# The last 1024 columns of a load as three loads of 96, 24 and 8 rows, in an add + GELU kernel on Trainium2

## The chip, the cores and the metric

The kernel runs on one core of a Trainium2 chip. The metric is the device time of one execution in microseconds (us), the median of several runs. Of the core's engines, four matter here: VectorE (DVE in the profile), ScalarE (ACT), GpSimd (POOL) and SyncE (SP), which only issues DMAs in this kernel. 16 DMA engines move data between HBM, where the inputs and the output lie, and SBUF, the memory that the engines work on, which has 128 rows (partitions).

## What is computed

Two float32 arrays of 1024 x 4096 are added, and the sum goes through the tanh form of GELU:

```python
z = x + y
return 0.5 * z * (1 + np.tanh(np.sqrt(2 / np.pi) * (z + 0.044715 * z ** 3)))
```

That is 33.55 MB read and 16.78 MB written.

## The kernel before, in words

Each array is seen as 128 rows of 32768 columns (L88): row p holds eight consecutive rows of the array, so a row's columns are contiguous in HBM. `zt` in SBUF holds a whole array (128 KB a row) and `yt` half of one (64 KB a row). Six DMAs, each of 128 rows by 16384 columns (64 KB a row, 8.39 MB), move everything, and all are issued by SyncE in this order (L169 to L171):

1. y, first half, into `yt` (load_y, L135)
2. x, first half, into `zt` (load_x, L130)
3. x, second half, into `zt` (L130)
4. y, second half, into `yt`, over the first half; it waits until all adds of the first half have read `yt`
5. store of the first half of `zt` (L139), after its last GELU
6. store of the second half, after its last GELU

The first two are moved ahead of the program's starting barrier (`begin_early`, L9), and the end of the program waits for the last store apart from everything else (`wait_late`, L23).

The work between is cut into 20 chunks of columns, mostly 2048 wide (L94); the last three are of 1024, 512 and 512. For each chunk an add makes z = x + y in place in `zt` (L150), on VectorE or, for chunks 7, 8 and 12, on GpSimd; then ScalarE applies GELU in place (L162). For eight chunks ScalarE first copies x into PSUM (L143), and the add reads it from there (`copies`, L95). The order on every engine is written out by hand (L96 to L98, L169 to L174), and a semaphore ends each wait. A DMA engine works off its share of the DMAs in the order in which they were issued.

Which loads a chunk waits for is worked out from the column ranges of the loads (`over`, L111, and `needs`, L176). The two functions that matter for the change:

```python
xloads = [HALF, HALF]                                     # L91
def load_x(i):                                            # L128
    a, b = xr[i]
    nc.sync.dma_start(out=zt[:, a:b], in_=xv[:, a:b])     # L130
```

Of the kernel before, what the change touches and what calls it, by code (L numbers as in the profile page):

```python
# [66 lines left out]
def kernel(  # L67
# [12 lines left out]
    nc = tc.nc  # L80
    P = nc.NUM_PARTITIONS
# [6 lines left out]
    xv, yv, ov = (a.rearrange("(p n) d -> p (n d)", p=P) for a in (x, y, out))  # L88

    HALF = TOT // 2  # L90
    xloads = [HALF, HALF]  # L91
    yloads = [16384, 16384]
    stores = [16384, 16384]
    chunks = [1024, 1024] + [2048] * 7 + [512, 1536] + [2048] * 6 + [1024, 512, 512]  # L94
# [6 lines left out]
    def ranges(sizes):  # L101
        ends = [sum(sizes[: i + 1]) for i in range(len(sizes))]
        assert ends[-1] == TOT
        return [(e - f, e) for e, f in zip(ends, sizes)]

    xr, yr, sr, cr = (ranges(r) for r in (xloads, yloads, stores, chunks))
# [4 lines left out]
    def over(rs, lo, hi):  # L111
        return [i for i, (a, b) in enumerate(rs) if a < hi and b > lo]
# [6 lines left out]
    zt = pool_sb.tile([P, TOT], fp32, tag="z", name="z")  # L119
# [7 lines left out]

    def load_x(i):  # L128
        a, b = xr[i]
        nc.sync.dma_start(out=zt[:, a:b], in_=xv[:, a:b])  # L130

    def load_y(i):
        a, b = yr[i]
# [30 lines left out]
    def earlier_user(c):  # L164
        lo, hi = copies[c], copies[c] + chunks[c]
        before = [k for k in copies if k < c and copies[k] < hi and copies[k] + chunks[k] > lo]
        return [(add, k) for k in before]

    sp = [(load_y, i) for i in over(yr, 0, HALF)] + [(load_x, 0), (load_x, 1)]  # L169
    sp += [(load_y, i) for i in over(yr, HALF, TOT)]  # L170
    sp += [(store, i) for i in range(len(stores))]  # L171
    pool = [(add, c) for c in on_gpsimd]
# [4 lines left out]
        load_x: lambda i: [],  # L177
        load_y: lambda i: [(add, c) for c in over(cr, yr[i][0] - HALF, yr[i][1] - HALF)],
        copy: lambda c: [(load_x, i) for i in over(xr, *cr[c])] + earlier_user(c),
        add: lambda c: [(load_x, i) for i in over(xr, *cr[c])]  # L180
        + [(load_y, i) for i in over(yr, *cr[c])]
        + [(copy, k) for k in copies if k == c]
# [56 lines left out]
```

## Time and profile before

| what | value |
|---|---|
| median of 3 runs | 120.08 us (119.96 to 120.28) |
| profiled execution, first to last instruction (span) | 118.7 us; no other time of it is given |
| VectorE busy | 29.1 us (25%) |
| ScalarE busy | 44.1 us (37%) |
| GpSimd busy | 13.8 us (12%) |
| adds, 128x2048, both operands in SBUF, VectorE | 2.28 us each |
| GELUs, 128x2048 | 1.90 us each |
| SyncE waits before its issue of the second y load | 53.2 us |
| SyncE waits before the two stores | 41.9 us in all, the longest 21.9 |

The page of a profile shows one execution: busy time of each engine, the span in 40 equal slices (each digit is the busy share in tenths; the DMA row is the mean over the 16 DMA engines), the DMA queues with their packets, the chain of work that ended last, and groups of instructions. The chain is followed back from the last instruction: at each step to what released it. Behind the page lies the trace. It lists each instruction, each update of a semaphore, and each DMA packet with its start, its duration and its size, though not the DMA engine that moved it. Where a landing is given, it is the time from the issue of a DMA to the last update of its semaphore.

### The profile page before, as it was taken

To read this page: it belongs to the slowest core of one execution; us is meant where nothing else is said; L and a number is where in the kernel's file an instruction comes from. 1 tells how busy PE (TensorE), PEld (TensorE's weight loads), DVE (VectorE), ACT (ScalarE), POOL (GpSimd) and SP (SyncE) were. 2 spreads that over 40 slices of the span, in tenths; PEclk is the share of its full clock that TensorE was granted. 3 is DMA by queue.
4 is the path that set the end of the run, shared out by engine and by line. 5 is a ranking of instruction groups with operands and counts; after the bars stand their busy time and mean duration, and the time that the engine had idled before them with its cause. 6 is when DMAs were issued, how large, how long until landed. Compare 5 with 4: busy or idle time off the path is not lost.

```text
span 118.7 us, 112 instructions
## 1 busy us (share of the span) xinstructions
DVE 29.1 (25%) x18; ACT 44.1 (37%) x30; POOL 13.8 (12%) x7
## 2 busy tenths in 40 slices
DVE  0000000000000099994000000009999920000000
ACT  5000000000000096792059999903799980000000
POOL 0000000000000029980000000009500000000000
DMA  9889988998899888998899888998899888988891
GB/s 353 353 375 641 398 353 353 596 464 353 353 420 618 376 353 353 618 442 353 353 508 552 353 353 375 641 398 353 353 552 508 353 353 353 707 353 353 353 641 66
DMA packets 864, 50.33 MB, mean 424 GB/s; under 512 B 96, under 2 KB 96, under 8 KB 96
## 3 DMA queue, kind: packets, MB, share of 16 engines
q1 hardware_dynamic: 864, 50.33, 98.5%
HBM read 33.55 MB, written 16.78 MB: 424 GB/s over the span
## 4 chain that ended last, share of the span: by engine, by line
DMA 56%; DVE 14%; ACT 10%; DVEq 1%; ACTq 0%; SPq 0%; issue 0%
DMA z<-in_x_dram 34%; DMA y<-in_y_dram 21%; DVE z L150 14%; ACT z L162 10%; DVEq L206 1%; ACTq L206 0%; SPq L135 0%; DVEq L150 0%
## 5 line engine op out<-in xcount | busy, mean ns | idle before, releaser
L162 ACT ACTIVATE z<-z 128x2048 f32<-128x2048 f32 (+3 forms) x20 | 29.7, 1555 | 5.5 <-DVE z L150 5.5
L143 ACT COPY ps<-z 128x2048 f32<-128x2048 f32 (+2 forms) x8 | 13.0, 1654 | 46.8 <-DMA z<-in_x_dram 45.1
L150 DVE TENSOR_TENSOR z<-z,y 128x2048 f32<-128x2048 f32 (+2 forms) x9 | 13.6, 1574 | 40.0 <-DMA z<-in_x_dram 40.0
L150 DVE TENSOR_TENSOR z<-ps,y 128x2048 f32<-128x2048 f32 (+2 forms) x8 | 15.6, 2016 | 25.4 <-DMA y<-in_y_dram 25.4
L150 POOL TENSOR_TENSOR z<-z,y 128x2048 f32<-128x2048 f32 x3 | 13.5, 4529 | 70.7 <-DVE z L150 43.4
L191 ACT ACT_TABLE_LOAD x1 | 1.3, 1283 | 1.3 <-PEq L223 1.3
L190 DVE MEMSET one<- 128x1 f32 x1 | 0.1, 59 | 1.3 <-PEq L223 1.3
L191 ACT ACTIVATE one<-one 128x1 f32<-128x1 f32 x1 | 0.2, 203 | 0.0
L223 POOL MEMSET const-float32-0.0<- 128x1 f32 x1 | 0.1, 99 | 0.2 <-issue 0.2
L223 POOL MEMSET const-bfloat16-1.0<- 128x1 bf16 x1 | 0.1, 102 | 0.0
L223 POOL MEMSET const-uint8-127<- 128x1 uint8 x1 | 0.1, 102 | 0.0
L223 POOL MEMSET const-float32-1.0<- 128x1 f32 x1 | 0.1, 99 | 0.0
## 6 DMA issues: line engine op xcount, KB each, us to landing
y<-in_y_dram SPq DMA_DIRECT2D x2, 23.6
z<-in_x_dram SPq DMA_DIRECT2D x2, 50.1
out_dram<-z SPq DMA_DIRECT2D x2, 21.6
```

The lines of the kernel that those rows point to most:

```text
L143: nc.scalar.copy(out=in_psum(c), in_=zt[:, a:b])
L150: ins = eng.tensor_add(out=zt[:, a:b], in0=first, in1=yt[:, o : o + b - a])
L162: nc.scalar.activation(out=zt[:, a:b], in_=zt[:, a:b], func=act.Gelu_apprx_tanh)
L190: nc.vector.memset(one[:, :1], 0.0)
L191: nc.scalar.activation(out=one[:, :1], in_=one[:, :1], func=act.Gelu_apprx_tanh)
L206: tc.compile()
L223: nc = _bacc.Bacc("TRN2", target_bir_lowering=False, num_devices=1)
```

## The change

The second x load is cut into a load of 15360 columns and a rest of 1024 columns. The load of 15360 columns still has all 128 rows (60 KB a row). The rest is issued as three DMAs of 96, 24 and 8 rows, with 4 KB a row, before the second y load:

```diff
     HALF = TOT // 2
-    xloads = [HALF, HALF]
+    xloads = [HALF, 15360, 1024]
...
     def load_x(i):
         a, b = xr[i]
-        nc.sync.dma_start(out=zt[:, a:b], in_=xv[:, a:b])
+        parts = [(0, P)] if b - a > 1024 else [(0, 96), (96, 120), (120, P)]
+        for f, e in parts:
+            nc.sync.dma_start(out=zt[f:e, a:b], in_=xv[f:e, a:b])
...
-    sp = [(load_y, i) for i in over(yr, 0, HALF)] + [(load_x, 0), (load_x, 1)]
+    sp = [(load_y, i) for i in over(yr, 0, HALF)] + [(load_x, 0), (load_x, 1), (load_x, 2)]
```

On SyncE the one issue becomes four, with no wait among them; no other engine's instructions move. The add of chunk 18 (512 columns), its GELU and the second store wait for the three small loads; everything else of the second half waits for the load of 15360 columns or for none. Two things follow from the number of DMAs: the first copy of the second half waits for the shorter load, and GpSimd clears the semaphores at the end in two instructions instead of one (L47).

## The prediction

> **What bounds the kernel now.** I read the table in 40 slices first, then the queue totals, then the chain that ended last in order of time, then the issues on SyncE with their landings, and last the packet records of the trace, listed by start.
>
> The page, its slices and queue totals:
>
> ```profile
> span 118.7 us, 112 instructions
> ...
> DMA  9889988998899888998899888998899888988891
> ...
> DMA packets 864, 50.33 MB, mean 424 GB/s; under 512 B 96, under 2 KB 96, under 8 KB 96
> ...
> q1 hardware_dynamic: 864, 50.33, 98.5%
> ```
>
> The DMA row is never below 8 until the last slice, and the packets fill 98.5% of the 16 DMA engines' time: six transfers of 8.39 MB, one behind the other, with no hole. The 864 packets are 768 of 64 KB (one row of a transfer each) and 96 of 4 bytes, one for each DMA engine and transfer. So a transfer is 128 rows, 8 for each of 16 DMA engines.
>
> The chain that ended last (start us, us, what), and the stores' line (issue to landing):
>
> ```profile
> 0.43 40.89 DMA z<-in_x_dram
> ...
> 41.42 13.37 DVE z L150 x7
> ...
> 54.86 25.15 DMA y<-in_y_dram
> ...
> 84.72 11.86 ACT z L162 x7
> ...
> 97.09 0.52 ACT z L162
> ```
>
> ```profile
> L139 SPq DMA_DIRECT2D out_dram<-z x2: 343/346/348, 77.2 to 97.6; - x2
> ...
> DMA to landing us min/median/max: 21.0/21.6/22.2
> ```
>
> The first x load lands at 0.43 + 40.89 = 41.3, the second y load at 80.0, the stores at 77.2 + 22.2 = 99.4 and 97.6 + 21.0 = 118.6, where the span ends. These landings lie about 19.3 us apart, however early the transfer was issued. The chain runs through VectorE and ScalarE only because each issue waits for them: the second y load is issued at 54.9, while the x load before it moves until 60.7; the last store at 97.6, while the first store moves until 99.4.
>
> The packet records say how tight that is. A 64 KB packet takes 2.418 us, and packets on one DMA engine start 2.414 to 2.417 us apart (27.1 GB/s); 8 x 2.414 = 19.31 is the spacing above. A DMA engine that is late stays late: at the first full packets they start 0.716 us apart from first to last, at the last packets 0.478 us. The last 4-byte packet starts at 118.31, its signal comes at 118.64. One place has a little slack of its own: the last store's first packets start at 98.49, 0.88 after its issue at 97.61, and three of the DMA engines waited some 0.1 us for it; the latest one didn't wait. So the time is that of the DMA engine that ends last, and everything in this forecast is about how many ns that one gains or loses.
>
> **The change, part by part.**
>
> SyncE. One x load becomes four, so three more issues. The timeline has 0.33 to 0.42 us for one of SyncE's issues: they end near 1.6 + 3 x 0.4 = 2.8 us. The next thing on SyncE is the second y load, which waits for the adds until 54.8: 52 us hide them. If that cover were gone, they would cost some 1.2 us.
>
> Waits that move. The main part of the second x load is 15360 of 16384 columns, so it lands 1024 / 16384 x 19.3 = 1.2 us earlier, near 59.5, and ScalarE's copies (start 60.74) with it. ScalarE then ends its seven long gelus 1.2 us sooner and the first store is issued near 76 instead of 77.2; it stands in the queue behind the second y load until 80, so nothing comes of it. VectorE's adds after that wait for the y load at 80.0, as before. The three small loads (near 60.7 to 62) are waited for by the second last add of 512 columns, near 95, and by the last store: over 30 us of cover. GpSimd has one more clearing of semaphores at the end, which waits for all but the last store; that store moves for 19 us beside it.
>
> Bytes. None more or less. But eight rows of 64 KB a DMA engine become eight of 60 KB and, for 128 rows of 4 KB, new shares. A 4 KB row at the rate above is 2.414 / 16 = 0.151 us. Whole rows in equal numbers mean 6 rows on each of 16 DMA engines for the 96; for the 24, which 16 does not divide, 2 rows on 12 (or 3 on 8); for the 8, 1 row on 8. I take 12 and 8: 6 + 2 + 1 = 9 rows on eight of them, 8 on four, 6 on four, where all had 8. No row of before shows a load of fewer rows; the bounds are equal shares still (0) and 6 + 3 + 1 = 10 rows (+0.302).
>
> What limits a DMA engine is the open question, and it sets the sign. In every transfer of before, a DMA engine works on its own eight rows, so 27.1 GB/s can be the limit of the engine or that of the place in SBUF which those eight rows share. Both fit every packet here.
>
> - If the engine is the limit: +0.151 us for nine rows, 0 for eight, -0.302 for six. This is the lower bound.
> - If the place is the limit, 27.1 GB/s for each group of eight rows: 24 rows are three groups' worth and 8 rows one, and a second DMA engine on the same group gains nothing. With groups of eight consecutive rows, the 96, the 24 and the 8 would each take 8 x 0.151 = 1.207 us for a DMA engine that has part in all three: 3.62 where it had 1.207, so +2.41. This is the upper bound.
>
> Between +0.15 and +2.41 no row of before is nearer to one end. Groups so scattered that 8 consecutive rows meet eight of them are as special as groups wholly in a block; I take the middle, **+1.28**, for the most delayed DMA engines. Both ends stay in the range.
>
> [...]
>
> Small packets. Three more transfers bring up to three more 4-byte packets (9 ns each) to a DMA engine, and eight more row packets. What a packet costs beside its bytes is not seen; nothing below, and the 9 ns of the 4-byte packet above: 0 to 0.1 us; I take 0.05.
>
> Who is last. If the late DMA engines are those with six rows, the delayed ones start from up to 0.48 us of lead. That is worth 0 to 0.4; I take 0.2 off.
>
> No cover remains behind this: all three transfers that follow are full, so a lag goes to the end unchanged. The second y load lands later by it, the adds, the gelus and the last store's issue too, and the first store ends later by the same, so the 0.88 us from issue to first packet stays covered as now.
>
> Sum: 1.28 + 0.05 - 0.20 = +1.13 us. The profiled execution has 118.68 from its first to its last instruction, and no other time of it is given; 119.8 is the span I expect. The median of the three runs is 120.08, so I count 1.4 us around the span, unchanged: 120.08 + 1.13 = **121.2 us**.
>
> **The rivals.**
>
> *The engine is the limit and the shares fit (the other side).* The place is the end of the last transfers: the last four DMA engines end 0.282, 0.385, 0.394 and 0.478 us behind the first, the other twelve within 0.214. If those four are the ones with six rows they come to 0.176 at most, and the nine-row ones, if they are the eight earliest, to 0.099 + 0.151 = 0.250: the end moves from 0.478 to 0.250, -0.23 us, and with 0.05 for packets -0.18: 119.9. It decides as soon as the late four are the lightened four; if instead a late one has nine rows, it is +0.15 + 0.05: 120.3. For it: a clean step in the records between twelve and four. Against it: no record says which DMA engine is which, and the limit must be wholly the engine's.
>
> *The change does not do what it says.* Each row stays with the DMA engine that has it in a full load; then all keep eight rows, and only the packets remain: +0.05, 120.1. For it: one engine on its own eight rows is all that before shows.
>
> *Place-bound and worse.* Rows dealt out in an order in which the DMA engines crowd on one group at a time: the upper bound and more, +2.4 to +4: 122.5 to 124. Against it: it needs them to be in step, while the records show them up to 0.7 us apart.
>
> **Chances.** Place-bound as summed 0.57, own range 120.7 to 122.0; engine-bound 0.28 (119.85 to 120.35); equal shares 0.08 (120.1); crowded 0.07. The range takes the first three: 119.85 to 122.0. A measurement of this kernel tells about 0.3%, 0.36 us, from no change: beyond 120.44 slower, under 119.72 faster. Faster: even the best balance is -0.23, so only what I have not thought of, 0.04. Same: most of engine-bound, equal shares and a small part of the first, 0.33. Slower: 0.63.
>
> **What would show it.** Landings: the second y load at 81.1 instead of 80.0 and both stores later by as much say place-bound; 79.8 to 80.2 says engine-bound or equal shares. In the packet records, 4 KB packets of 0.3 us or longer say that a destination is shared; 0.151 to 0.16 that it isn't. Their count by DMA engine shows the shares. The spread of the last packets, 0.478 now, grows beyond 0.8 if the nine-row engines are held up and shrinks to 0.25 if the shares fit. It would all be wrong if a hole opened in the DMA row near 60 us, or if the last store were issued after the first one's end.

## The result, and the profile after

The changed kernel takes 121.28 us (median of 4 runs, 121.11 to 121.49) against 120.16 us for the kernel before in the same comparison (119.96 to 120.28). The ratio is 1.0099, with a 95% interval of 1.0087 to 1.0111: 1.0 to 1.3 us slower.

The page of the changed kernel:

```profile
span 119.9 us, 121 instructions
...
DMA  9899888998899799799699988998899888988890
...
DMA packets 1028, 50.33 MB, mean 420 GB/s; under 512 B 132, under 2 KB 132, under 8 KB 260
...
q1 hardware_dynamic: 1028, 50.33, 98.5%
```

The bytes are the same, the span is 1.2 us longer, and the packets still fill 98.5% of the DMA engines' time. No hole opened, so the packets themselves became longer. The count tells the shares: 640 rows of 64 KB, 128 of 60 KB, 128 of 4 KB, and 132 packets of 4 bytes, which is 7 transfers x 16, 12 for the load of 24 rows and 8 for the load of 8 rows.

The chain of the changed kernel in order of time (start us, us, what), its loads of y, and its stores:

```profile
0.43 40.84 DMA z<-in_x_dram
...
54.81 26.46 DMA y<-in_y_dram
...
98.36 0.52 ACT z L164
```

```profile
L141 SPq DMA_DIRECT2D out_dram<-z x2: 343/358/372, 76.4 to 98.9; - x2
...
DMA to landing us min/median/max: 21.0/22.6/24.2
```

The first x load lands at 41.3, as before. The second y load lands at 54.81 + 26.46 = 81.27 (before 80.01), the first store at 76.4 + 24.2 = 100.6 (99.4), the last at 98.9 + 21.0 = 119.9 (118.6). All of the loss lies between 41 and 81 us; after that every landing is simply 1.2 us later.

The packet records narrow it down. Rows of 60 KB take 2.267 us, as their size asks. The 4 KB rows take 0.159 us until 59.0 us, then 0.17 to 0.43, with a mean of 0.225 over all 128. The 64 KB rows right behind them, the first of the second y load, take 2.59 to 3.41 us instead of 2.418. From then on nearly every row takes 2.418 again (2.54 at most). A few records of the changed kernel, in order of start (start ns, duration ns, bytes):

```
58398  159   4096
59015  173   4096
59184  282   4096
59803 3408  65536
60407  316   4096
60631  431   4096
61348 2589  65536
63151 2424  65536
```

### The profile page after: what moved, and what is told of

It reads as the page before. It is cut to its first block, busy times and chain, and to the rows that moved or that the text cites. A ratio compares the mean times of both kernels' runs of the same rounds, so it can differ in the third digit from the quotient of the medians.

```text
span 119.9 us, 121 instructions
## 1 busy us (share of the span) xinstructions
DVE 29.1 (24%) x18; ACT 44.1 (37%) x30; POOL 13.8 (11%) x7
## 3 DMA queue, kind: packets, MB, share of 16 engines
q1 hardware_dynamic: 1028, 50.33, 98.5%
## 4 chain that ended last, share of the span: by engine, by line
DMA 56%; DVE 13%; ACT 10%; DVEq 2%; issue 1%; ACTq 0%; SPq 0%
DMA z<-in_x_dram 34%; DMA y<-in_y_dram 22%; DVE z L152 13%; ACT z L164 10%; DVEq L208 2%; ACTq L208 0%; SPq L137 0%; DVEq L152 0%; ACTq L164 0%
## 6 DMA issues: line engine op xcount, KB each, us to landing
y<-in_y_dram SPq DMA_DIRECT2D x2, 24.2
```

## The experiments

Theory PLACE is the forecast's: DMA engines that write to the same place of SBUF share that place's 27.1 GB/s (64 KB in 2.418 us). Which rows share a place, no run shows for single rows; a load is called crowded below where it has neighbouring rows that are only a part of the 128. Its rivals: SHARES, only the unequal count of rows matters; SMALL, rows of 4 KB are slow by themselves. All ratios below are against the kernel before, with a 95% interval, and us are worked out with its 120.1. An edit that takes lines away starts from the changed kernel, one that only adds lines from the kernel before, where nothing else is said.

### One load of all 128 rows

```diff
-        parts = [(0, P)] if b - a > 1024 else [(0, 96), (96, 120), (120, P)]
+        parts = [(0, P)]
```

> Only the cut of the columns is left: the last 1024 columns come in one load of all 128 rows, 8 rows of 4 KB on every DMA engine. Theory PLACE (DMA engines that write the same few places of SBUF share the 27.1 GB/s of that place): no engine meets another, so only packets are paid, +0.05 to +0.15 us over before, and no 4 KB packet above 0.17 us. Rival SMALL (rows of 4 KB, and the restart of long rows behind them, are slow by themselves, whichever engine has them): 4 KB packets of 0.25 us again and +1.0 to +1.2 us. Rival SHARES (nine rows instead of eight): 0 to +0.1.

Ratio 1.0063 (1.0046 to 1.0081), +0.6 to +1.0 us: outside what PLACE allows. But the records give SMALL no support: all 128 packets of 4 KB take exactly 0.159 us, and the 64 KB rows behind them 2.418. From the start of the last 60 KB row to the start of the first 64 KB row a DMA engine needs 3.519 us on average, of which 2.264 are the 60 KB row: 1.255 for eight small rows and their ends, where 1.207 is their share of bytes. So the small rows cost 0.05 us. The rest of the loss is made elsewhere: in the last rows of the second y load, which start at 76.6 to 77.1 and take 2.66 to 3.42 us each. Nothing like it stands in the changed kernel. What it is was a question of its own (theory EARLY, below).

### Two loads of 64 rows

```diff
-        parts = [(0, P)] if b - a > 1024 else [(0, 96), (96, 120), (120, P)]
+        parts = [(0, P)] if b - a > 1024 else [(0, 64), (64, P)]
```

> The last 1024 columns come in two loads of 64 rows, rows 0 to 63 and 64 to 127: 4 + 4 rows on every DMA engine, equal shares. PLACE: each load reaches half of the places, 8 rows of 0.151 us on each, so 1.207 + 1.207 us where one load of 128 rows has 1.207: +1.0 to +1.3 us. SHARES: nothing is unequal, +0.05 to +0.1. SMALL: +1.0 to +1.2, as in the run with one load.

Ratio 1.0084 (1.0053 to 1.0115), +0.6 to +1.4 us; PLACE's range. Shares are equal here, four rows and four, and the first store, issued at 76.0, leaves the last rows of the second y load at 2.44 us or less; but the 4 KB packets take 0.240 us on average (up to 0.346), the 64 KB rows behind them 2.84. The unequal shares are not needed for the loss; that a load reaches only a part of the rows is enough. The chain's line for the second y load:

```profile
54.56 26.32 DMA y<-in_y_dram
```

### Twice the bytes in the same three loads

```diff
-    xloads = [HALF, 15360, 1024]
+    xloads = [HALF, 14336, 2048]
-        parts = [(0, P)] if b - a > 1024 else [(0, 96), (96, 120), (120, P)]
+        parts = [(0, P)] if b - a > 2048 else [(0, 96), (96, 120), (120, P)]
```

> The three loads of 96, 24 and 8 rows are kept and take the last 2048 columns instead of 1024 (8 KB a row, as many packets). PLACE: the lag grows with the bytes, +2.0 to +2.6 us over before. SMALL: as many packets and one restart, so the lag stays at +1.0 to +1.3. SHARES: +0.3.

Ratio 1.0232 (1.0202 to 1.0262), +2.4 to +3.1 us: its middle, +2.8, lies above PLACE's upper end of +2.6, and it is far from SMALL's and SHARES' values. The packets are as many and twice as large; the loss goes from 1.2 to 2.8. A cost per packet or per transfer would have stayed; why the loss more than doubles is not shown. The chain's line for the second y load:

```profile
54.87 28.18 DMA y<-in_y_dram
```

### The places one by one

```diff
     def load_x(i):
         a, b = xr[i]
+        if i == 0:
+            for f, e, s in [(0, 8, 1), (0, 32, 4), (0, 128, 16), (0, 8, 1), (0, 64, 4), (0, 16, 1), (0, 64, 1), (0, 128, 1)]:
+                nc.sync.dma_start(out=zt[f:e:s, a:b], in_=xv[f:e:s, a:b])
         nc.sync.dma_start(out=zt[:, a:b], in_=xv[:, a:b])
```

> The kernel before, with eight more loads of x rows (64 KB each, the same data as the first x load brings again later) put ahead of the first x load, each waiting for the one before to land: 8 rows from 0 in steps of 1 (behind the y load, not counted), then 8 rows in steps of 4, 8 in steps of 16, 8 in steps of 1, 16 in steps of 4, 16 in steps of 1, 64 in steps of 1, 128 in steps of 1. [...] SHARES (the limit is the engine's alone): every row has a DMA engine of its own in the five short loads, so all five take the same 2.4 us, the 64 rows 9.7 and the 128 rows 19.3.

Each of these loads is issued when the one before has landed, so the distance of two issues is the time of one load. The timeline of SyncE in this kernel, one execution, around each issue (start us, us of the issue, what), from the second of the eight on:

```profile
31.32 0.73 SPq L132 DMA_DIRECT2D z<-in_x_dram  x1
...
36.35 0.58 SPq L132 DMA_DIRECT2D z<-in_x_dram  x1
...
43.86 0.29 SPq L132 DMA_DIRECT2D z<-in_x_dram  x1
...
54.76 0.54 SPq L132 DMA_DIRECT2D z<-in_x_dram  x1
...
62.03 0.32 SPq L132 DMA_DIRECT2D z<-in_x_dram  x1
...
73.66 0.50 SPq L132 DMA_DIRECT2D z<-in_x_dram  x1
...
96.44 0.36 SPq L132 DMA_DIRECT2D z<-in_x_dram  x1
```

| load of 64 KB rows | issue to the next issue, us | first packet's start to last packet's end, us |
|---|---|---|
| 8 rows, steps of 4 | 5.0 | 3.2 |
| 8 rows, steps of 16 | 7.5 | 5.5 |
| 8 rows, steps of 1 | 10.9 | 9.0 |
| 16 rows, steps of 4 | 7.3 | 5.5 |
| 16 rows, steps of 1 | 11.6 | 9.5 |
| 64 rows | 22.8 | 20.8 |
| 128 rows | 21.8 (landing) | 20.5 |

The first three rows have the same number of rows, DMA engines, packets and bytes; only the distance of the rows differs, and the time goes from 3.2 to 9.0 us. If each DMA engine had its own 27.1 GB/s, they would be equal. Nor do the neighbouring rows wait for each other on one DMA engine: the eight rows in steps of 1 start within 0.12 us and last 7.6 to 8.9 us each, where the eight rows in steps of 4 last 2.8 to 3.2, so eight DMA engines work at once and each is slow. And 64 rows take as long as 128. That is PLACE without the rest of the kernel. Which rows share a place can be read from the times only as far as the loads go: rows 8 to 15 beside rows 0 to 7 cost 0.5 us more (9.0 to 9.5), rows 32 to 60 beside rows 0 to 28, in steps of 4, 2.3 us (3.2 to 5.5).

One thing these runs leave open. Row p of SBUF always gets row p of the array, so another distance in SBUF is another distance in HBM too. A cost that simply grows with the distance in HBM, or simply shrinks with it, does not fit: steps of 4 are the fastest, and both the closer and the wider rows are slower. But a limit in HBM that groups the rows in the same way would look alike, and no run moves a row to another place.

### Eight needless rows, apart and together

```diff
         nc.sync.dma_start(out=zt[:, a:b], in_=xv[:, a:b])
+        if i == 1:
+            nc.sync.dma_start(out=one[0:32:4, 32:992], in_=xv[0:32:4, 0:960])    # apart
+            nc.sync.dma_start(out=one[120:128, 32:992], in_=xv[120:128, 0:960])  # together
```

One of the two lines in each kernel, on top of the kernel before: eight rows of 3840 bytes into a tile that nobody reads, taken to be one row on each of eight DMA engines. The first line has the rows 0, 4, ... 28, which as rows of 64 KB moved in 3.2 us by themselves (steps of 4 in the table above), the second the neighbouring rows 120 to 127; eight neighbouring rows took 9.0 us there.

> [...] PLACE and SHARES alike: each of the eight engines gets 0.15 us more, so 0 to +0.2 us on the time, packets of 0.15 us.

> [...] SHARES: the same as for rows that lie apart, 0 to +0.2, packets of 0.15 us.

Apart: ratio 1.0004 (0.9995 to 1.0013), nothing in the time. Together: 1.0035 (1.0022 to 1.0047), +0.3 to +0.6 us. PLACE holds and SHARES falls: eight DMA engines with one row more than the others cost nothing that can be measured, the same rows in a heap do. The forecast's sign of a shared destination, small packets of twice their time (0.3 us for 4 KB), fails here: they last 0.149 us in both. With the rows together, the delay stands in the next packets: all sixteen 64 KB rows behind them last 0.19 to 0.33 us longer, 0.22 on average. Apart it is 0 to 0.17, 0.05 on average. The chain's line for the second y load, apart and then together:

```profile
54.72 25.36 DMA y<-in_y_dram
```

```profile
54.77 25.66 DMA y<-in_y_dram
```

### Where the single load lost its time

EARLY says: the cut lets ScalarE start earlier, the first store is issued earlier, and that holds up the DMA engines at the end of the second y load. FOURTH says that one more transfer costs it.

```diff
-    xloads = [HALF, 15360, 1024]
+    xloads = [HALF, 1024, 15360]   # one kernel
+    xloads = [HALF, 8192, 8192]    # another kernel
-        parts = [(0, P)] if b - a > 1024 else [(0, 96), (96, 120), (120, P)]
+        parts = [(0, P)]
```

> The one load of 1024 columns (all 128 rows) stands ahead of the load of 15360 columns instead of behind it, for its first columns. The second half of x is then complete no earlier than before, so ScalarE's copies and the first store's issue stand where they were before. It asks where the +0.6 to +0.8 us of the single load at the end came from, which has no crowded place. Theory EARLY (its profile has all DMA engines held up by 0.65 us in the last rows of the second y load, after the first store was issued 1.4 us earlier than before): the hold-up goes with the early issue, so +0.05 to +0.15 over before here. Rival FOURTH (one more load of small rows costs it, wherever it stands): +0.6 to +0.8 again.

> The second x load is cut into two loads of 128 rows by 8192 columns (32 KB a row, equal shares, no crowded place). x is half there some 9.7 us earlier, ScalarE starts earlier and the first store is issued many us ahead of the end of the second y load. EARLY: +0.5 us or more over before, with 64 KB packets above 2.6 us just ahead of the first store's. FOURTH with small rows as the cause: +0.02 to +0.1, no such packets.

Small load first: 1.0045 (1.0032 to 1.0059), +0.4 to +0.7 us, between the two theories; its first store is issued at 76.5, still 0.7 us earlier than before, which I had not expected, and twelve of its last y rows are 0.26 to 0.70 us too long. Half the columns: 1.0072 (1.0055 to 1.0088), first store at 71.2, last y rows 0.54 to 0.93 us too long. The second is in EARLY's range, but both kernels have one load more than the kernel before, so neither decides. The next two do, one with the load and without the early issue, one with the early issue and without the load, which leaves out chunk 8's GELU:

```diff
     def gelu(c):
         a, b = cr[c]
+        if c == 8:                          # the single load at the end, store later
+            for _ in range(2):
+                nc.scalar.activation(out=one[:, :992], in_=zt[:, :992], func=act.Gelu_apprx_tanh)
```

> The single load of 1024 columns at the end again, with two needless GELUs of 992 columns (about 1.0 us each) on ScalarE ahead of the last GELU of the first half, so that the first store is issued 2 us later, near 77.8 as in the kernel before, still ahead of the end of the second y load. EARLY (the single load's cost is a hold-up that an earlier issue of the first store brings): +0.05 to +0.2 over before, and no 64 KB packet above 2.6 us near 77. FOURTH (the extra load's cost comes by another way): +0.6 to +0.8 stays.

```diff
     def gelu(c):
         a, b = cr[c]
+        if c == 8:                          # the kernel before, store earlier
+            return
```

> The kernel before with the GELU of chunk 8 left out (those 2048 columns are stored as x + y), so that the first store is issued 1.9 us earlier, near 75.3; the six DMAs are unchanged. EARLY: +0.5 to +0.8 over before with slow 64 KB packets near 77. FOURTH: 0.

The single load with the late store: 0.9995 (0.9986 to 1.0005). The kernel before with the early store: 1.0081 (1.0062 to 1.0100), +0.7 to +1.2 us, the middle above the +0.5 to +0.8 that EARLY gave. FOURTH falls; EARLY holds for these kernels. Of the single load, the chain's line for the second y load and the stores' line:

```profile
54.64 25.92 DMA y<-in_y_dram
```

```profile
L141 SPq DMA_DIRECT2D out_dram<-z x2: 343/345/347, 75.7 to 98.2; - x2
```

Of the single load with the late store, the same two:

```profile
54.71 25.20 DMA y<-in_y_dram
```

```profile
L141 SPq DMA_DIRECT2D out_dram<-z x2: 344/346/348, 77.8 to 97.5; - x2
```

Of the kernel before with the early store:

```profile
54.66 25.98 DMA y<-in_y_dram
```

```profile
L139 SPq DMA_DIRECT2D out_dram<-z x2: 343/346/348, 75.2 to 98.3; - x2
```

The y load, issued at the same time in all three, lands 0.7 to 0.8 us later where the store was issued at 75.2 or 75.7 than where it was issued at 77.8. No load's bytes or rows differ between the kernel before and the last of these. With 77.0 and 77.2 there was no loss in the time either (eight rows apart; the kernel before).

### Is that in the changed kernel too?

The same two edits in the changed kernel: two needless GELUs, or chunk 8's GELU left out.

> The changed kernel with the same two needless GELUs ahead of the last GELU of the first half: its first store is issued near 78.4 instead of 76.4, with the second y load under way until 80 to 81. PLACE: the lag is made at 59 to 63 us and nothing is slow at the first store, so nothing changes, +1.0 to +1.2 over before. EARLY as a part of the changed kernel's time: +0.5 to +0.7, as the rest would go.

> The changed kernel with the GELU of chunk 8 left out (those 2048 columns are stored as x + y): its first store is issued 1.9 us earlier, near 74.5, some 5.5 us ahead of the end of the second y load. It asks whether the changed kernel is free of the hold-up that an early first store brought to the kernel before (+0.9 us). EARLY added to PLACE: +1.8 to +2.1 over before, with slow 64 KB packets near 77.6. If the changed kernel is free of it for another reason: +1.0 to +1.2 as without.

Store at 78.2: 1.0092 (1.0075 to 1.0109). Store at 74.3: 1.0094 (1.0061 to 1.0126). With the changed kernel's own 76.4 it was 1.0099. The time doesn't move, and in none of the three profiles is a last row of the second y load longer than 2.44 us. So the changed kernel's loss is made at 59 to 63 us and has nothing of EARLY in it. The chain's line for the second y load and the stores' line, with the late store:

```profile
54.75 26.34 DMA y<-in_y_dram
```

```profile
L141 SPq DMA_DIRECT2D out_dram<-z x2: 344/358/372, 78.2 to 98.7; - x2
```

With the early store:

```profile
54.70 26.32 DMA y<-in_y_dram
```

```profile
L141 SPq DMA_DIRECT2D out_dram<-z x2: 343/357/371, 74.3 to 98.7; - x2
```

Beside the single load with a late store (25.20, time 120.07 against 121.22) this is the cleanest pair of the study: the same columns cut off, the same needless GELUs, stores issued at 77.8 and 78.2, and nothing else but 96 + 24 + 8 rows against 128. It puts the price of the crowded places at 26.34 - 25.20 = 1.14 us in the chain and 1.15 us in the time. Why the changed kernel doesn't suffer from an early store is open. The two loads of 64 rows, with a store at 76.0, and the three loads with twice the bytes, with one at 75.4, don't either, so the crowding seems to take the hold-up's place; what the DMA engines do differently then, no record shows.

## Why the prediction was right

- **The bound.** Right. The time is that of the DMA engine that ends last; a lag made at 60 us is found unchanged in all three landings behind it (+1.26, +1.30 and +1.27 us, by the last updates of the semaphores).
- **SyncE's issues.** Right: the five x loads were issued from 0.4 to 2.7 us with at most 0.52 us each, 50 us ahead of the next thing on SyncE.
- **Waits that move.** Right in the outcome for this kernel: the first store was issued at 76.4, and nothing came of it. ScalarE's copies began 0.77 us earlier (59.97 instead of 60.74), not 1.2. The reason given was too short. That the store "stands in the queue behind the second y load" was taken as no cost, and in the kernel before a store issued 2.0 us earlier cost 0.97 us. That nothing came of it here goes with the crowded loads, which the forecast did not know: as far as the forecast goes, this zero was luck.
- **Shares.** 12 DMA engines for 24 rows and 8 for 8, as taken: the semaphores of these loads count 12 and 8 landings at the end, and the 4-byte packets say the same.
- **Engine or place.** Place, as forecast. The size, +1.28 as the middle of +0.15 and +2.41: from the start of the last 60 KB rows to that of the second 64 KB rows a DMA engine needs 7.13 us on average, in the kernel with one load of 128 rows 5.93. That is 1.19 us. The forecast had worked out the two bounds and not the size between them, so that the middle comes within 0.1 is in part luck. Of the signs, the landing of the second y load came as said (81.27, forecast 81.1), while the 4 KB packets, 0.225 us on average and 0.431 at most, stayed mostly under the 0.3 that was to say that a destination is shared. The forecast says that both ends stay in the range, but the upper one does not: with +2.41 the sum gives 122.3, and the range ends at 122.0.
- **Small packets.** 0.05 taken, 0.05 measured.
- **Who is last.** 0.20 taken off; too much. The last DMA engine ended 0.32 us behind the mean in the kernel before (offsets of the last packets, mean 0.155, last 0.478) and 0.28 after (0.107 and 0.384): 0.05. The reason was wrong too. The forecast had the nine-row engines delayed and the others less, and a spread above 0.8 at the end; it is 0.384. All sixteen ended some 1.2 us late. The engines that came early to the second y load lost there what they had gained: 3.41 us for the first y row of the earliest, 2.59 for that of the latest. By PLACE they met the stragglers of the small loads in their own places; the records, which do not name the engines, fit that but do not show it.
- **The sum.** 1.28 + 0.05 - 0.20 = 1.13; in the records 1.19 + 0.05 - 0.05 = 1.19. Two errors of 0.1 and 0.15 cancel in part.
- **The rivals.** That the engine is the limit falls with the places one by one, and so does "it does not do what it says": the loads of 24 and 8 rows ran on 12 and 8 DMA engines, and in the places one by one eight neighbouring rows moved at once, not one after the other. The crowded case of +2.4 and more did not come.

## What to carry to other kernels

In a kernel whose DMA engines are never idle, ask not only how many rows each DMA engine gets but which rows are written at the same time: here a load of 64 neighbouring rows took as long by itself as one of all 128 (20.8 and 20.5 us), and a crowded load of 8 rows delayed what stood behind it on every DMA engine (0.19 to 0.33 us). A balance of shares that was put at 0.23 us at best wasn't worth loads of neighbouring rows that cover only a part of the 128: they cost 1.0 to 1.3 us here. And when a cut lets another engine finish earlier, look at what it then issues: a store that only waited in the queue, issued 2.0 us earlier, cost 0.97 us here.

## What the runs showed of the hardware

- 64 rows of 64 KB took 20.8 us, 128 rows 20.5: half the rows, no time saved.
- Eight rows of 64 KB took 3.2 us in steps of 4, 5.5 in steps of 16 and 9.0 in steps of 1, from first start to last end: 164, 95 and 58 GB/s. Sixteen rows took 5.5 us in steps of 4 and 9.5 in steps of 1.
- A crowded load of 8 rows of 3840 bytes (120 to 127) lengthened all sixteen rows that came next, one on each DMA engine, by 0.19 to 0.33 us.
- A store issued 1.35 us ahead of the last row of the load in front of it (the kernel before with the early store) lengthened that row by 0.5 to 1.1 us on every DMA engine; issued as that row was under way (77.0 to 77.8 us, other kernels), it lengthened at most four of the sixteen by 0.10 to 0.18 us, and the time not measurably. Earlier was not worse (71.2: 0.54 to 0.93). What happens there is open.
